# Two layers of a hybrid decoder on one core: parameter loads, a gate, a value half, the turnings and the warm-up put at other places

## The chip, the core and the metric

The kernel runs on one core of one Trainium2 chip. The time is that of the device in microseconds (us); runs of the same kernel are compared by their median. Five engines work beside each other, each through its own instructions in order: TensorE (PE: matmuls; PEld: the loading of their stationary operand), VectorE (DVE), ScalarE (ACT), GpSimd (POOL) and SyncE (SP), which here issues every DMA.

## What is computed

The input is 512 positions of width 1024 in float32. Two layers follow each other, each with `x <- LayerNorm(alpha * x + sublayer(x))`.

The first, even layer projects x to six parts (q, k, v, a gate g_ret, and xb, g_lru) and has two branches:

```
q, k = rope(q), rope(k) * dk**-0.5                # 8 heads of 128
ret  = (q k^T * decay) v                          # per head, causal
ret  = groupnorm(ret) * gn_g + gn_b;  ret *= silu(g_ret)
xc   = causal_conv4(xb)
r, i = sigmoid(xc Wa + ba), sigmoid(xc Wx + bx)   # 8 diagonal blocks
a    = exp(-8 r softplus(-lam));  u = xc i sqrt(1 - a^2)
lru  = scan(h = a h + u) * silu(g_lru)
y    = concat(ret, lru) W_out
```

The second, odd layer is differential attention with 8 heads, two softmax maps each:

```
w   = softmax(q1 k1^T) - lambda softmax(q2 k2^T)  # causal
out = rmsnorm(w v) * subln_g * (1 - lambda_init) * silu(g)
y   = out W_out
```

## The kernel before, in words

**Numbers.** Every matmul operand of weight is a pair: a rounded high part (`h`, cast by ScalarE) and the remainder (`l`, subtracted by VectorE). `split` (L140) makes such a pair, and `mm3` (L149) multiplies two pairs with three matmuls, high by high, high by low and low by high. So a product needs first the high parts and then the low ones.

**Weights.** They come in pieces of 128 x 1024 (512 KB), in the order of the list `order`, and are numbered w0, w1, ... in the profile. `fetch` (L164) loads the next piece into one of two raw buffers and splits it into one of five pairs; a raw buffer is free again when VectorE has made the low part. `take` (L179) hands out the next piece and fetches ahead. The arrays on the host are laid out in the same order (`layout`, L731).

**Units.** TensorE's main work is in units of 24 matmuls or 96: `t_unit` (a weight piece times all of x, result transposed: q, k, xb, and the gates gl and gr of the even layer), `s_unit` (four pieces, result by position: the values and the odd layer's gate og) and `out_unit` (the output projections: out, lo, ro, eo, oo). The even layer's order is the list `ev` (L249): for each pair of heads gl, xb, gr, q, k of the first head and then of the second, with the first half of the values (v 0, heads 0 to 3) ahead of all and the second half (v 1, heads 4 to 7) between xb 4 and gr 4. v 0 goes piece by piece; v 1 is "major": it takes its four pieces at once and goes position block by position block, and each block is evicted by `evac` (L415).

**Side work.** What a head does beside the projections is a generator: `retention` (L432), `lru` (L475), `attention` (L598), and the turning of the normalized rows (`fin`, L574). `Side` (L47) holds them as jobs. After each mm3 of a main unit one tick is counted (`side.tick`), and at each tick the first job that is due and within its group's limit runs one step, up to its next `yield n`, which makes it due n ticks later. TensorE's and SP's instructions stand in the program exactly in this order. Where a main unit needs a job's result, `side.need` puts the clock of ticks forward to the job's times and runs its steps at once, with no main matmuls in between. ScalarE's, VectorE's and GpSimd's instructions are ordered by a planner that goes by priorities.

Steps that the change and the prediction speak of:

- In `retention`: four scores `rs` (jb 0 to 3; 512, 384, 256, 128 columns) into two PSUM banks `ps_sc`, each multiplied by the decay into `rsd` and split; the product `ro` with the values; its square `rq`, split; after RET_NORM ticks the mean square `rv` through a matmul with `ones`; then the group norm and the gate. A head is in `seen` once its `ro` is in the program. Before v 1, the loop waits with `need` until heads 0 to 3 are in `seen` (L535), because v 1 is written over v 0's tiles.
- In `lru`: the convolution (xbp, xc); after LRU_GATES ticks the two gate products `pr` and `pi` at once, both into `ps_sc`; sigmoid of both (L492, L496), a tanh (L498), and so on to the scan.
- In `attention`, for one head and one block of 128 queries (qb): the scores `as` of the two maps, a masked maximum and exponentials; after ATT_SCORES ticks the turning `wt` of the weights; after ATT_TURN ticks the product `po` with the values, in the only bank of `ps_av`; a square sum (L638), its inverse root on GpSimd (L326, L327), the scaling to `o` on VectorE (L642); after ATT_NORM ticks two transposes (the turning of o, L646) into the free half of the same bank, split into `om`. ATT_FREE = 2 ticks later the next `po` may start. A head's blocks start at least ATT_GAP ticks apart (8; for the last head 7), three at a time.
- `ln_params` (L362) loads gain and offset of a normalization, broadcast over the partitions, in four halves of 256 KB. For the even layer that is at L568, behind `ident` and ahead of the last four weights of the layer (w60 is fetched already, w61 to w63 are not); the buffers are those of two decay tiles and of the gate weights.
- The start (L278 to L300): seven dummy matmuls on `ones`, then x and the first pieces, in turns.

Of the kernel before, what the change touches and what calls it, by code (L numbers as in the profile page):

```python
# [14 lines left out]
P = 128  # L15
D = 1024
S = 512
KT = D // P
SB = S // P
HALF = 512  # L20
# [12 lines left out]
ATT_START, ATT_GAP = (12,) * 7 + (7,), (8,) * 7 + (7,)  # L33
ATT_SCORES = (7, 7, 7, 9)
ATT_TURN = (4, 3, 4, 4)
ATT_NORM = 5
ATT_FREE = 2
ATT_VALUE = 2

P_ROPE, P_SCORES, P_SQUARE, P_GROUP, P_VALUE = 50, 13, 60, 5, 60  # L40
P_CONV, P_GATES = 9, 5
P_LN, P_LAST, P_WEIGHTS, P_ATT = 10, 10, 450, 337
WARM_UP = 7
EARLY = 2


# [50 lines left out]
def trunk(ctx: ExitStack, tc: tile.TileContext, a):  # L97
    nc = tc.nc
# [20 lines left out]
    side = Side()  # L119
# [17 lines left out]
    def cut(t, *ix):  # L137
        return t[0][ix], t[1][ix]
# [7 lines left out]
        nc.scalar.copy(out=dst[0], in_=src)  # L146
        nc.vector.tensor_tensor(out=dst[1], in0=src, in1=dst[0].bitcast(F32), op=ALU.subtract)

    def mm3(out, l, r, start, stop):  # L149
        nc.tensor.matmul(out=out, lhsT=l[0], rhs=r[0], start=start, stop=False)  # L150
        nc.tensor.matmul(out=out, lhsT=l[0], rhs=r[1], start=False, stop=False)  # L151
        nc.tensor.matmul(out=out, lhsT=l[1], rhs=r[0], start=False, stop=stop)  # L152

# [5 lines left out]

    ew, ow, eo, oo = a["ev_w"], a["od_w"], a["ev_wo"], a["od_wo"]  # L160
    order, ready = [], []
    extra, stats = {}, {}

    def fetch(parts=((0, D),)):  # L164
        if len(ready) < len(order):
            n = len(ready)
            src, scale = order[n]
            raw = wraw.tile([P, D], F32, tag="raw", name=f"w{n}_r")
            w = pair(extra.pop(n, wsp), [P, D], "w", f"w{n}")
            for lo, hi in parts:  # L170
                c = slice(lo, hi)
                nc.sync.dma_start(out=raw[:, c], in_=src[:, c])
                split(raw[:, c], cut(w, ALL, c), scale=scale)
                yield
            ready.append(w)

    taken = [0]
# [15 lines left out]
    def s_unit(act, name, major, evac, before=None):  # L193
        def product(ps, w, sb, kt):
            j = kt % 2 * HALF
            mm3(ps, cut(act, ALL, kt, slice(sb * P, sb * P + P)), cut(w, ALL, slice(j, j + HALF)), kt == 0, kt == KT - 1)
            if kt == KT - 1:
                evac(sb, ps)
            side.tick()

        if major:
            with tc.high_priority(P_WEIGHTS):
                ws = [take(0) for _ in range(KT // 2)]
            for sb in range(SB):
                before(sb)
                ps = bank(ps_pj, "pj", f"{name}_ps{sb}")
                for kt in range(KT):
                    product(ps, ws[kt // 2], sb, kt)
        else:
            ps = [bank(ps_pj, "pj", f"{name}_ps{sb}") for sb in range(SB)]  # L210
            for i in range(KT // 2):
                w = take(2)
                steps = [(sb, j) for sb in range(SB) for j in range(2)]
                if taken[0] == 1:

                    steps.sort(key=lambda t: t[1])
                for sb, j in steps:
                    product(ps[sb], w, sb, 2 * i + j)
# [30 lines left out]
    ev = [("v", 0)]  # L249
    for p in range(3):  # L250
        one, two = (2 * p, 2 * p + 1)
        ev += [("gl", one), ("xb", one)] + [("v", 1)] * (p == 2) + [("gr", one), ("q", one), ("k", one)]
        ev += [("gl", two), ("xb", two)] + [("out", p - 1)] * (p > 0) + [(n, two) for n in ("gr", "q", "k")]
    ev += [("xb", 6), ("q", 6), ("k", 6), ("lo", 2), ("xb", 7), ("q", 7), ("k", 7)]
    ev += [("gr", 6), ("gl", 6), ("gr", 7), ("gl", 7), ("ro", 2)]
# [26 lines left out]
    ones = const.tile([P, P], F32R, tag="ones", name="ones")  # L282
    nc.vector.memset(ones.bitcast(F32), 1.0 / P)
    idle = bank(ps_tp, "tp", "idle")
    for _ in range(WARM_UP):
        nc.tensor.matmul(out=idle, lhsT=ones, rhs=ones.unsqueeze(1).to_broadcast([P, 4, P]), start=True, stop=True)

    x = pair(big, [P, KT, S], "x", "x")
    xr = big.tile([P, KT, S], F32, tag="y", name="xr")
# [69 lines left out]
            nc.vector.scalar_tensor_tensor(out=hv[hf], in0=hv[hf], scalar=rs, in1=gb[1][hf], op0=ALU.mult, op1=ALU.add)  # L359
            yield hf, hv[hf]  # L360

    def ln_params(src, name, *slots):  # L362
        slots = iter(slots)
        return [[load(f"{name}{r}{hf}", [P, HALF], src[r:r + 1, hf * HALF:hf * HALF + HALF].partition_broadcast(P), *next(slots))
                 for hf in range(2)] for r in range(2)]


    phase = ctx.enter_context(ExitStack())
# [43 lines left out]
    def v_even(i):  # L412
        out = []

        def evac(sb, ps):  # L415
            with tc.high_priority(P_VALUE):
                p3 = ps.rearrange("p (h e) -> p h e", e=P)
                m = small.tile([P, 4], F32, tag="vm", name="vm")
                nc.vector.tensor_reduce(out=m, in_=p3, axis=AX.X, op=ALU.add)
                nc.vector.tensor_scalar(out=m, in0=m, scalar1=1.0 / P, scalar2=None, op0=ALU.mult)  # L420
                c = work("vc")
                nc.vector.tensor_tensor(out=c.rearrange("p (h e) -> p h e", e=P), in0=p3, in1=m.unsqueeze(2).broadcast_to([P, 4, P]), op=ALU.subtract)
                t = pair(vp, [P, S], "v", f"ev{i}{sb}")
                split(c, t)
            out.append(t)

        s_unit(x, f"ev{i}", i == 1, evac, lambda sb: None)
        return out
# [46 lines left out]
    def lru(c, ps, m):  # L475
        with tc.high_priority(P_CONV):
            xb = temp(f"xbp{c}")
            nc.scalar.copy(out=xb, in_=ps)
            xc = temp(f"xc{c}")
            nc.scalar.activation(out=xc, in_=ps, func=AF.Identity, scale=conv_w(3, c), bias=conv_b(c))  # L480
            for w in range(3):
                sh = 3 - w
                nc.vector.scalar_tensor_tensor(out=xc[:, sh:], in0=xb[:, :S - sh], scalar=conv_w(w, c), in1=xc[:, sh:], op0=ALU.mult, op1=ALU.add)  # L483
        with tc.high_priority(P_GATES):
            t2 = part(S, f"xc{c}")
            split(xc, t2)
        yield LRU_GATES[c]
        pr = bank(ps_sc, "sc", f"pr{c}")
        o = c % 2 * 2 * P
        mm3(pr, cut(gw[0], ALL, slice(o, o + P)), t2, True, True)  # L490
        t = temp(f"t{c}")
        nc.scalar.activation(out=t, in_=pr, func=AF.Sigmoid, bias=gba(c))  # L492
        pi = bank(ps_sc, "sc", f"pi{c}")
        mm3(pi, cut(gw[0], ALL, slice(o + P, o + 2 * P)), t2, True, True)
        i = xb
        nc.scalar.activation(out=i, in_=pi, func=AF.Sigmoid, bias=gbx(c))  # L496

        nc.scalar.activation(out=t, in_=t, func=AF.Tanh, scale=sp4[:, c:c + 1])  # L498
        nc.vector.tensor_tensor(out=i, in0=i, in1=xc, op=ALU.mult)  # L499
        d = xc  # L500
        r = temp(f"r{c}")

        nc.scalar.activation(out=r, in_=t, func=AF.Ln, bias=1.0)
        nc.scalar.activation(out=r, in_=r, func=AF.Exp, scale=-1.0)  # L504
        nc.vector.scalar_tensor_tensor(out=d, in0=t, scalar=1.0, in1=r, op0=ALU.add, op1=ALU.mult)  # L505
        nc.vector.scalar_tensor_tensor(out=d, in0=d, scalar=2.0, in1=r, op0=ALU.subtract, op1=ALU.mult)
        nc.scalar.activation(out=r, in_=t, func=AF.Sqrt)
        nc.vector.scalar_tensor_tensor(out=t, in0=t, scalar=1.0, in1=d, op0=ALU.subtract, op1=ALU.mult)
        nc.vector.scalar_tensor_tensor(out=r, in0=r, scalar=-2.0, in1=d, op0=ALU.mult, op1=ALU.mult)
        nc.vector.tensor_tensor(out=r, in0=r, in1=i, op=ALU.mult)  # L510
        nc.vector.tensor_tensor_scan(out=d, data0=t, data1=r, initial=0.0, op0=ALU.mult, op1=ALU.add)
        if ("gl", c) not in gates:
            yield lambda: 0 if ("gl", c) in gates else math.inf
        nc.vector.tensor_tensor(out=d, in0=d, in1=gates.pop(("gl", c)), op=ALU.mult)
        split(d, cut(m, ALL, c % 2))
# [17 lines left out]

    for kind, i in ev:
        if kind == "v":  # L535
            if i:
                for j in range(4):
                    side.need(job["ret", j], lambda: j in seen)
            v = v_even(i)
        elif kind == "xb":  # L540
            if i % 2 == 0:
# [23 lines left out]
    for i in (6, 7):  # L565
        side.need(job["lru", i])
    ident = load("ident", [P, P], a["ident"])
    gb0 = ln_params(a["ev_ln"], "ln0", (two, "dec"), (two, "dec"), (two, "gwh", 1), (two, "gwl", 1))  # L568
    h = pair(big, [P, KT, S], "x", "h")

    def even_end(sb):
# [26 lines left out]
    def attention(hd, qb, q, k, m):  # L598
# [37 lines left out]
        with tc.high_priority(P_ATT):  # L636
# [3 lines left out]
            rsqrt(ss, rs, 1.0 / (2 * P), zr[:, 1:2])  # L640
            o = es.tile([P, 2 * P], F32, tag="o", name=f"o{hd}{qb}")
            nc.vector.scalar_tensor_tensor(out=o, in0=po[:, :2 * P], scalar=rs, in1=gates[qb, hd // 2][:, hc:hc + 2 * P], op0=ALU.mult, op1=ALU.mult)  # L642
        yield ATT_NORM
        pm = po[:, 2 * P:]
        for i in range(2):
            nc.tensor.transpose(out=pm[:, i * P:i * P + P], in_=o[:, i * P:i * P + P], identity=ident)  # L646
# [27 lines left out]
    for kind, i in od:  # L674
# [31 lines left out]
                oj[i, qb] = side.add(attention(i, qb, *qk, om[i]), "att", 3, ATT_START[i], ATT_GAP[i])  # L706
        else:
            odd_out(i, f"oo{i[0]}")
    gb1 = ln_params(a["od_ln"], "ln1", *((qkp, n) for n in ("qh", "ql", "kh", "kl")))
    odd_out((6, 7), "oo6", after=odd_end, late=P_LAST)  # L710


# [18 lines left out]
def layout(i):  # L731
# [13 lines left out]
    for p in range(4):  # L745
        for h in (2 * p, 2 * p + 1):
            names = (wl, wx, wg, wq, wk) if p < 3 else (wx, wq, wk)
            part = [t_pieces(m[:, h * P:h * P + P]) for m in names]
            if h == 0:
                part.insert(0, s_pieces(wv[:, :HALF]))  # L750
            if h == 4:
                part.insert(2, s_pieces(wv[:, HALF:]))
            ev += part
    ev += [t_pieces(m[:, h * P:h * P + P]) for h in (6, 7) for m in (wg, wl)]
    w = i["od_w_in"][0]
# [38 lines left out]
```

## Time and profile before

| | |
|---|---|
| median of 3 runs | 938.7 us (938.13 to 939.02) |
| the profiled execution | 939.08 us, span 937.3 us |
| PE busy | 922.1 us, 4327 matmuls |
| DVE, ACT, POOL busy | 703.2, 450.6, 60.5 us |
| granted TensorE clock, mean | 0.997 |
| HBM read, written | 86.09 MB, 2.10 MB |

The span goes from the first to the last instruction of the profiled execution. In a timeline's row stand the start, the time taken, the engine, the line, the operation, and the tile written with the tiles read; "x2" means that two such instructions are merged. In brackets stands how long the engine was idle before, and the instruction that ended it. In a row of the waits stand the waiting engine and line, what it waited for, and the total, the number of times and the longest. `SPq` is SP issuing a DMA.

### The profile page before, as it was taken

What the parts mean: (1) busy time and instruction counts of PE and PEld (TensorE: products, weight loads), DVE (VectorE), ACT (ScalarE), POOL (GpSimd) and SP (SyncE); (2) the same over time, 40 slices, a digit from 0 to 9 for tenths busy, and PEclk for the clock granted to TensorE, in tenths of its full rate; (3) what the DMA queues carried; (4) which work ended last, traced back from release to release, by engine and by line L of the source; (5) the groups of instructions that cost most, each with busy time, mean ns of one, the idle gap of its engine ahead of it and who ended that gap; (6) DMA issues with size and microseconds to landing.
All of it is one profiled execution on the core that took longest, in us unless ns stands there. A gap on an engine that the chain in (4) does not pass through costs nothing.

```text
span 937.3 us, 11561 instructions
## 1 busy us (share of the span) xinstructions
PE 922.1 (98%) x4327; PEld 765.1 (82%) x4327; DVE 703.2 (75%) x1187; ACT 450.6 (48%) x740; POOL 60.5 (6%) x118
## 2 busy tenths in 40 slices
PE   9999999999999999999999999999999999999996
PEld 7888888878888887788888888888888888888885
DVE  6877997868769987994589864578764488647677
ACT  5567786566484776423334443233443234434240
POOL 0000000000000000000001210100110101101023
PEclk9999999999999999999999999999999999999998
DMA  6562221512314123405222122142222142223102
GB/s 226 179 215 68 88 75 53 168 57 90 124 41 161 57 90 115 124 3 188 90 91 68 68 88 73 43 133 92 69 68 90 45 135 68 69 90 112 67 23 91
DMA packets 27416, 88.94 MB, mean 95 GB/s; under 512 B 3424, under 2 KB 3552, under 8 KB 27360
## 3 DMA queue, kind: packets, MB, share of 16 engines
q1 hardware_dynamic: 27360, 88.20, 28.4%
q8 instruction: 34, 0.56, 0.2%
q14 instruction: 22, 0.18, 0.1%
HBM read 86.09 MB, written 2.10 MB: 94 GB/s over the span
## 4 chain that ended last, share of the span: by engine, by line
PE 74%; DVE 14%; ACT 6%; issue 3%; POOL 1%; DMA 1%; SPq 0%; DVEq 0%; ACTq 0%; POOLq 0%
PE ov_ps L152 3%; PE ov_ps L151 3%; PE ov_ps L150 3%; PE og_ps L150 3%; PE og_ps L152 3%; PE og_ps L151 3%; PE oo_ps L150 3%; PE oo_ps L151 2%; PE oo_ps L152 2%; PE ev_ps L150 2%; PE ev_ps L151 2%; PE ev_ps L152 2%; PE xb_ps L150 1%; PE xb_ps L151 1%; PE xb_ps L152 1%
## 5 line engine op out<-in xcount | busy, mean ns | idle before, releaser
L611 ACT ACTIVATE e<-as,nm 128x128 f32<-128x128 f32 (+3 forms) x64 | 33.1, 523 | 25.3 <-DVE nm L608 25.2
L642 DVE SCALAR_TENSOR_TENSOR o<-po,ars,og 128x256 f32<-128x256 f32 x32 | 15.5, 484 | 36.1 <-POOL ars L327 35.1
L618 POOL TENSOR_SCALAR zr<-z 128x1 f32<-128x1 f32 x32 | 13.4, 419 | 311.3 <-ACT e L611 311.3
L608 DVE CUSTOM_DVE_ANT_0 as<-as,mask 128x128 f32<-128x128 f32 (+3 forms) x64 | 30.2, 510 | 1.5 <-PE as L152 1.5
L326 POOL TENSOR_SCALAR rs_t<-bmv 128x1 f32<-128x1 f32 x6 | 2.2, 374 | 420.5 <-DVE bmv L337 420.5
L638 ACT ACTIVATE po<-po 128x256 f32<-128x256 f32 x32 | 11.9, 372 | 25.8 <-PE po L152 25.4
L326 POOL TENSOR_SCALAR rs_t<-ss,zr 128x1 f32<-128x1 f32 x32 | 14.9, 467 | 131.1 <-ACT po L638 126.0
L327 POOL TENSOR_TENSOR ars<-rs_t,nhalf 128x1 f32<-128x1 f32 x32 | 20.6, 644 | 2.7
L240 DVE TENSOR_TENSOR y<-oo_ps,y 128x512 f32<-128x512 f32 x24 | 16.4, 685 | 4.2 <-PE oo_ps L152 4.2
L483 DVE SCALAR_TENSOR_TENSOR xc<-xbp,vecs,xc 128x509 f32<-128x509 f32 (+2 forms) x24 | 17.9, 746 | 1.8 <-ACT xc L480 1.6
L619 DVE SCALAR_TENSOR_TENSOR e<-e,zr,e 128x128 f32<-128x128 f32 (+3 forms) x32 | 17.6, 551 | 0.9
L440 DVE TENSOR_TENSOR rsd<-rs,dec 128x512 f32<-128x512 f32 (+3 forms) x32 | 15.5, 486 | 1.0 <-PE rs L152 0.8
L646 PEld LDWEIGHTS po<-ident,o 128*128 128x128 f32 x64 | 8.3, 140 | 7.4 <-DVE o L642 4.5
L697 DVE SCALAR_TENSOR_TENSOR og<-og,og_ps 128x512 f32<-128x512 f32 x16 | 10.9, 686 | 4.3 <-ACT og L696 4.3
L623 PE MATMUL wt<-ident,e 128*128 128x128 f32 x80 | 13.9, 272 | 0.0
L646 PE MATMUL po<-ident,o 128*128 128x128 f32 x64 | 12.6, 278 | 1.1 <-DVE o L642 0.8
L696 ACT ACTIVATE og<-og_ps 128x512 f32<-128x512 f32 x16 | 9.6, 598 | 8.0 <-PE og_ps L152 7.7
L623 PEld LDWEIGHTS wt<-ident,e 128*128 128x128 f32 x80 | 10.5, 140 | 3.5
L146 ACT CAST hh<-ht 128x512 fp32r<-128x512 f32 x8 | 4.7, 588 | 17.5 <-PE ht L578 17.5
L499 DVE TENSOR_TENSOR xbp<-xbp,xc 128x512 f32<-128x512 f32 x8 | 5.5, 690 | 9.7 <-ACT xbp L496 9.7
L611 ACT ACTIVATION_READ_ACCUMULATOR e<-as,nm 128x1 f32 x64 | 12.6, 196 | 0.0
L505 DVE SCALAR_TENSOR_TENSOR xc<-t,r 128x512 f32<-128x512 f32 x8 | 5.5, 690 | 9.0 <-ACT r L504 9.0
(2672 smaller groups left out, 3409.3 us busy)
## 6 DMA issues: line engine op xcount, KB each, us to landing
w_r<-in_od_w SPq DMA_DIRECT2D x64, 512.0 KB, 3.3
w_r<-in_ev_w SPq DMA_DIRECT2D x47, 512.0 KB, 3.3
w_r<-in_ev_wo SPq DMA_DIRECT2D x16, 512.0 KB, 3.3
w_r<-in_od_wo SPq DMA_DIRECT2D x16, 512.0 KB, 3.3
dec<-in_dec SPq DMA_DIRECT2D x8, 256.0 KB, 3.8
y<-in_x SPq DMA_DIRECT2D x4, 512.0 KB, 6.7
out_h<-y SPq DMA_DIRECT2D x8, 256.0 KB, 2.1
xr<-in_xt SPq DMA_DIRECT2D x3, 512.0 KB, 6.9
```

The lines of the kernel that those rows point to most:

```text
L150: nc.tensor.matmul(out=out, lhsT=l[0], rhs=r[0], start=start, stop=False)
L151: nc.tensor.matmul(out=out, lhsT=l[0], rhs=r[1], start=False, stop=False)
L152: nc.tensor.matmul(out=out, lhsT=l[1], rhs=r[0], start=False, stop=stop)
L240: nc.vector.tensor_tensor(out=yy, in0=ps, in1=yy, op=ALU.add)
L326: nc.gpsimd.tensor_scalar(out=t, in0=var, scalar1=scale, scalar2=eps, op0=ALU.mult, op1=ALU.add)
L327: nc.gpsimd.tensor_tensor(out=out, in0=t, in1=nhalf[:, :1], op=ALU.pow)
L483: nc.vector.scalar_tensor_tensor(out=xc[:, sh:], in0=xb[:, :S - sh], scalar=conv_w(w, c), in1=xc[:, sh:], op0=ALU.mult, op1=ALU.add)
L608: nc.vector.tensor_tensor_reduce(out=ps[:, :n], in0=ps[:, :n], in1=mask[:, S - n:], scale=-QK_SCALE, scalar=3.0e38, op0=ALU.add, op1=ALU.m ...
L611: nc.scalar.activation(out=e, in_=ps[:, :n], func=AF.Exp, scale=-1.0, bias=nm, accum_out=z[:, mp:mp + 1])
L619: nc.vector.scalar_tensor_tensor(out=ee[0], in0=ee[1], scalar=zr[:, 0:1], in1=ee[0], op0=ALU.mult, op1=ALU.add)
L623: nc.tensor.transpose(out=pt[:, kb * P:kb * P + P], in_=ee[0][:, kb * P:kb * P + P], identity=ident)
L646: nc.tensor.transpose(out=pm[:, i * P:i * P + P], in_=o[:, i * P:i * P + P], identity=ident)
```

## The change

- The even layer's four parameter halves are no longer loaded together. `fetch` has a list `behind`: after a piece is fetched, what is listed for its number is run. The first half is listed behind the next piece, the second behind the one after it, the third and fourth behind the third.
- In `lru` a `yield 1` stands between `pr` and `pi`.
- In `ev`, for the pair p = 2, gr 4 comes ahead of v 1 (and so in `layout`). The `need` for heads 0 to 3 moves from before the value unit into its first eviction, which comes after eight of its mm3.
- ATT_NORM is 5, 6, 6, 6 for the query blocks 0 to 3 instead of 5 for all.
- WARM_UP is 8 instead of 7, and in the first mm3 of the kernel one more dummy matmul, of 256 columns, stands between the first and the second matmul (`between`).
- The odd layer's parameters are loaded as before, by another expression.

```diff
-ATT_NORM = 5
+ATT_NORM = (5, 6, 6, 6)
...
-WARM_UP = 7
+WARM_UP = 8
...
-    def mm3(out, l, r, start, stop):
+    def mm3(out, l, r, start, stop, between=lambda: None):
         nc.tensor.matmul(out=out, lhsT=l[0], rhs=r[0], start=start, stop=False)
+        between()
         nc.tensor.matmul(out=out, lhsT=l[0], rhs=r[1], start=False, stop=False)
...
-    extra, stats = {}, {}
+    extra, behind, stats = {}, {}, {}
...
                 split(raw[:, c], cut(w, ALL, c), scale=scale)
                 yield
+            for then in behind.pop(n, ()):
+                then()
             ready.append(w)
...
             j = kt % 2 * HALF
-            mm3(ps, cut(act, ALL, kt, slice(sb * P, sb * P + P)), cut(w, ALL, slice(j, j + HALF)), kt == 0, kt == KT - 1)
+            between = {"between": lambda: busy_pe(2)} if (taken[0], sb, kt) == (1, 0, 0) else {}
+            mm3(ps, cut(act, ALL, kt, slice(sb * P, sb * P + P)), cut(w, ALL, slice(j, j + HALF)), kt == 0, kt == KT - 1, **between)
...
-        ev += [("gl", one), ("xb", one)] + [("v", 1)] * (p == 2) + [("gr", one), ("q", one), ("k", one)]
+        ev += [("gl", one), ("xb", one), ("gr", one)] + [("v", 1)] * (p == 2) + [("q", one), ("k", one)]
...
+    def busy_pe(n):
+        nc.tensor.matmul(out=idle[:, :n * P], lhsT=ones, rhs=ones.unsqueeze(1).to_broadcast([P, n, P]), start=True, stop=True)
+
     for _ in range(WARM_UP):
-        nc.tensor.matmul(out=idle, lhsT=ones, rhs=ones.unsqueeze(1).to_broadcast([P, 4, P]), start=True, stop=True)
+        busy_pe(4)
...
-    def ln_params(src, name, *slots):
-        slots = iter(slots)
-        return [[load(f"{name}{r}{hf}", [P, HALF], src[r:r + 1, hf * HALF:hf * HALF + HALF].partition_broadcast(P), *next(slots))
-                 for hf in range(2)] for r in range(2)]
+    def ln_param(src, name, r, hf, slot):
+        return load(f"{name}{r}{hf}", [P, HALF], src[r:r + 1, hf * HALF:hf * HALF + HALF].partition_broadcast(P), *slot)
...
         def evac(sb, ps):
+            if i and sb == 0:
+                for j in range(4):
+                    side.need(job["ret", j], lambda: j in seen)
...
         nc.scalar.activation(out=t, in_=pr, func=AF.Sigmoid, bias=gba(c))
+        yield 1
         pi = bank(ps_sc, "sc", f"pi{c}")
...
         if kind == "v":
-            if i:
-                for j in range(4):
-                    side.need(job["ret", j], lambda: j in seen)
             v = v_even(i)
...
-    gb0 = ln_params(a["ev_ln"], "ln0", (two, "dec"), (two, "dec"), (two, "gwh", 1), (two, "gwl", 1))
+
+    gb0 = [[None] * 2, [None] * 2]
+    for n, slot in enumerate(((two, "dec"), (two, "dec"), (two, "gwh", 1), (two, "gwl", 1))):
+        def param(r=n // 2, hf=n % 2, slot=slot):
+            gb0[r][hf] = ln_param(a["ev_ln"], "ln0", r, hf, slot)
+
+        behind.setdefault(len(ready) + min(n, 2), []).append(param)
...
-        yield ATT_NORM
+        yield ATT_NORM[qb]
...
-    gb1 = ln_params(a["od_ln"], "ln1", *((qkp, n) for n in ("qh", "ql", "kh", "kl")))
+    gb1 = [[ln_param(a["od_ln"], "ln1", r, hf, (qkp, n)) for hf, n in enumerate(ns)] for r, ns in enumerate((("qh", "ql"), ("kh", "kl")))]
...
             if h == 4:
-                part.insert(2, s_pieces(wv[:, HALF:]))
+                part.insert(3, s_pieces(wv[:, HALF:]))
```

## The prediction

> **What bounds the kernel now.** I read the page's first two parts first, for the engine that is full, then what this engine waited for, and then the timeline around each of its waits.
>
> ```profile
> span 937.3 us, 11561 instructions
> ...
> PE 922.1 (98%) x4327; PEld 765.1 (82%) x4327; DVE 703.2 (75%) x1187; ACT 450.6 (48%) x740; POOL 60.5 (6%) x118
> ```
>
> TensorE is busy for 98% of the span, so nothing but its gaps can be won: 937.3 - 922.1 = 15.2 us, of which the normalization after the last matmul takes most. What the gaps wait for:
>
> ```profile
> PE rv L457 <- ACT rq7h L146: 1.4, 1, 1.4
> ...
> PE po L646 <- DVE o L642: 0.8, 2, 0.4
> PE pi L150 <- DVE rsd L440: 0.7, 1, 0.7
> ```
>
> A busy time here includes the drain of the pipeline, which is longer than the distance between two matmuls, so a gap shows up too small. I therefore measure from start to start: two 512-column matmuls at full clock start 0.23 us apart, a 384-column one takes 0.17 and a 256-column one 0.12 by the same proportion. All that is above this is lost time. A "tick" below is what one call of side.tick stands beside: three such matmuls, 0.68 us.
>
> **Part 1, the start (two more dummy matmuls).**
>
> ```profile
> 1.07 3.36 PE L286 MATMUL idle<-ones 128*128 128x512 f32 x7 [1.07 <-DVE ones L283]
> 4.92 0.80 PE L150 MATMUL ev_ps<-w0h,xh 128*128 128x512 f32 x1 [0.50 <-ACT w0h L146]
> 5.65 0.80 PE L151 MATMUL ev_ps<-w0l,xh 128*128 128x512 f32 x1
> 9.22 0.63 PE L150 MATMUL ev_ps<-w0h,xh 128*128 128x512 f32 x1
> 9.65 0.45 PE L151 MATMUL ev_ps<-w0l,xh 128*128 128x512 f32 x1
> 11.43 1.23 DVE L147 TENSOR_TENSOR w1l<-w_r,w1h 128x1024 fp32r<-128x1024 f32 x1 [0.41 <-ACT w1h L146]
> 12.90 0.39 PE L150 MATMUL ev_ps<-w1h,xh 128*128 128x512 f32 x1
> 13.13 0.39 PE L151 MATMUL ev_ps<-w1l,xh 128*128 128x512 f32 x1
> ```
>
> Up to 9.65 us matmuls start 0.43 us apart (9.22 to 9.65), after it 0.23: TensorE runs at half speed until it has worked without a break from 5.65 on, 4.0 us. Seven dummies at 0.43 are issued by 1.07 + 3.0 = 4.1; an eighth ends at 4.5 and so lies in the idle time before 4.92. The dummy between the first two real matmuls has 256 columns, 0.21 us at the slow rate, and stands in the 0.73 - 0.43 = 0.30 us that the second one waits for w0l. Both cost nothing while these waits are there; without them 0.43 and 0.21. What they may bring is that the busy stretch counts from 1.07 instead of from 5.65, so that full speed comes some 4.6 us earlier. But the data don't come earlier: the second matmul on w1 needs w1l, done at 11.43 + 1.23 = 12.66. It started at 13.13, so at most 0.47 us is won, and a loss is excluded as long as the waits stay. Ends 0 and 0.47; I take **0.4**, since the idle time left in the stretch (4.5 to 4.92, and 0.1) is short against what there was. By the Trainium skill (TensorE: Matmul & The Clock Gate, section "What's actually happening") the gate opens after one busy window of about 3.4 us, and the window is free-running. The trace's 4.0 us agrees. By that rule other runs of the kernel before turn fast up to 12.5 us (estimate: 5.65 and two windows), 1.4 us worse than this one, and the sum below would be up to 1.4 us better.
>
> **Part 2, value half 1 after gr4, and its need inside the first eviction.** The stretch in which the loop forced head 3's steps, each without cover, and the nearest like pattern (head 1):
>
> ```profile
> 191.63 0.29 PE L152 MATMUL rs<-q3h,k3l 128*128 128x256 f32 x1
> 192.20 0.33 PE L150 MATMUL rs<-q3h,k3h 128*128 128x128 f32 x1 [0.28 <-DVE rsd L440]
> 193.34 0.33 PE L150 MATMUL ro<-r31h,ev01h 128*128 128x384 f32 x1
> 194.13 0.44 PE L151 MATMUL ro<-r31l,ev01h 128*128 128x384 f32 x1 [0.46 <-DVE r31l L147]
> ...
> 122.14 0.50 PE L457 MATMUL rv<-rq1h,ones 128*128 128x512 f32 x1
> 122.87 0.50 PE L458 MATMUL rv<-rq1l,ones 128*128 128x512 f32 x1 [0.23 <-DVE rq1l L147]
> ```
>
> Lost: 0.57 - 0.12 = 0.45 and 0.79 - 0.17 = 0.62, together 1.07. After the change head 3's scores come by their own times (yields of 4, 4, 4, 7): one in xb4, two in gr4, the last at tick 1 of the value unit, and the product ro would be due at tick 8, which is where the need now stands. So it forces at most that one step, after seven ticks of cover, and the 1.07 go. Nothing is moved in the sum of work; the four weights of this unit and gr4's change places, equal in size, and q4 takes gr4's place as the unit whose next weight comes late. What comes in: lru 4's gates, due 12 ticks after their convolution, fall on ticks 6 and 7 with ro at 8 and rv six ticks later. That is head 1's pattern, where the second rv came 0.73 - 0.23 = 0.50 late. Bounds of this cost: 0, and 1.0 (twice that row, as the value evictions also want ScalarE there). I take 0.5: net **0.6** won.
>
> **Part 3, pi a tick behind pr.** Eight moves; one of them stands at a wait:
>
> ```profile
> 304.23 0.40 PE L152 MATMUL pr<-xc6h,gw6l 128*128 128x512 f32 x1
> 304.72 0.56 DVE L440 TENSOR_TENSOR rsd<-rs,dec 128x384 f32<-128x384 f32 x1
> 305.33 0.50 PE L150 MATMUL pi<-xc6h,gw6h 128*128 128x512 f32 x1 [0.71 <-DVE rsd L440]
> ```
>
> pi waits for its bank, which the multiply at 304.72 frees at 305.28. Lost: 1.10 - 0.23 = 0.87. With a tick of main matmuls (0.68) in front, 0.2 is left: **0.67** won. The other seven cost TensorE nothing, they only change places with three matmuls. ScalarE does the tanh of pr's gate before pi's sigmoid in most of them (L498 ahead of L496), and that covers the tick; uncovered, each gate would come up to 0.68 later on ScalarE.
>
> **Part 4, the norm parameters one by one behind w61, w62, w63.**
>
> ```profile
> 356.47 10.46 SPq L156 DMA_DIRECT2D ln<-in_ev_ln  x4
> 367.04 8.72 SPq L172 DMA_DIRECT2D w_r<-in_ev_wo  x3
> ...
> 365.54 1.22 DVE L147 TENSOR_TENSOR w59l<-w_r,w59h 128x1024 fp32r<-128x1024 f32 x1
> ...
> 373.10 1.05 ACT L146 CAST w61h<-w_r 128x1024 fp32r<-128x1024 f32 x1 [6.64 <-DMA w_r<-in_ev_wo]
> ...
> 373.54 0.39 PE L152 MATMUL ro_ps<-w59h,retm2l 128*128 128x512 f32 x1
> 375.35 0.50 PE L457 MATMUL rv<-rq7h,ones 128*128 128x512 f32 x1 [1.42 <-ACT rq7h L146]
> 376.08 0.50 PE L458 MATMUL rv<-rq7l,ones 128*128 128x512 f32 x1 [0.22 <-DVE rq7l L147]
> ...
> w_r<-in_ev_wo SPq DMA_DIRECT2D x16, 512.0 KB, 3.3
> ```
>
> Four broadcasts of 256 KB stand in SP's queue before w61; the last are issued just ahead of it. w61 needs 6.06 us to 373.10, against a median of 3.3. ScalarE works in order, so the cast of w61 holds up head 7's square and cast, and with them rv: 1.81 - 0.23 = 1.58 and 0.73 - 0.23 = 0.50, together 2.08 lost. Moving the loads doesn't issue w61 much earlier, because its raw buffer is w59's, free at 365.54 + 1.22 = 366.76. What goes is the competition: landed after 3.3 us, w61 is there at 370.2, and cast, square and cast (some 2.4 us in all) end at 372.6, ahead of the 373.77 at which TensorE wants rv. The first parameter now follows w61 at once. If the two share the engines, w61 lands 0.7 us later (the excess of 6.06 - 3.3 = 2.8 spread over four loads) to 1.4 (over two); with 0.7 its low half and then rq7l still come in time, with 1.4 rq7l is 0.6 late. I take 0.2: **1.9** won, bounds 0.5 (the cast only half as much earlier) and 2.08. By the Trainium skill (DMA: Bandwidth & Descriptors, "Queues, rings and completion order") descriptors of one queue are consumed in ring order, which would make the later load harmless and the sum 0.2 better. Of what is queued behind the parameters on SP: w62, w63, lq and w64. The second parameter's slot is head 7's decay, whose last multiply is done before w59l, and the last two take lru 7's gate weights, long used; so none of them waits in the queue by then. The normalization that reads them comes after the whole first row of eo; if they were late there, up to their 3.9 us each could be lost.
>
> **Part 5, one tick more before the turning (query blocks 1 to 3).**
>
> ```profile
> 504.76 0.39 PE L152 MATMUL q20o_ps<-hh,w80l 128*128 128x512 f32 x1
> 505.23 0.44 PE L646 MATMUL po<-ident,o 128*128 128x128 f32 x2
> ...
> 675.56 0.39 PE L152 MATMUL og_ps<-w105h,hl 128*128 128x512 f32 x1
> 676.38 0.44 PE L646 MATMUL po<-ident,o 128*128 128x128 f32 x2 [0.42 <-DVE o L642]
> ...
> 866.83 0.19 PEld L150 LDWEIGHTS po<-ov30h,w63h 128*128 128x128 f32 x1 [0.47 <-DVE om6l L147]
> ```
>
> The turning waits for VectorE's o, which waits for GpSimd. Lost at 505: 0.47 - 0.23 = 0.24; at 676: 0.82 - 0.23 = 0.59. I find seven such places, two like the second (676, 806) and five of 0.21 to 0.25 (505, 515, 558, 666, 795), none of them in query block 0: 1.17 + 1.14 = 2.3. One tick, 0.68, is more than the longest. What it costs: the single bank of po is free one tick later. So the distance between two po of a head is 6 + 2 = 8 ticks, which is ATT_GAP; before it was 7. Counted through by hand, most heads keep their starts (a collision at tick 24 even lets the next head start a tick earlier), and head 1's four po come to stand right at the end of the bank's two free ticks, where the row at 866 shows a wait of about 0.2 us. Two of these four I count: 0.4. Bounds 0 and 0.8. Net **1.9** won.
>
> **Part 6, the end.** Head 7's turnings come 0, 1, 2 and 3 ticks later. Its last one stands at tick 43 of the drain and the last row of oo6 begins behind tick 49; 46 is in time.
>
> ```profile
> 917.00:929.00 12.00, 11.69 (x53) 9.32 (x51) 11.73 (x22) 1.14 (x2) 3.02 (x5) 1.00 0.13 48
> 917.10 0.48 DVE L642 SCALAR_TENSOR_TENSOR o<-po,ars,og 128x256 f32<-128x256 f32 x1 [1.60 <-POOL ars L327]
> ```
>
> The columns of the first row are stretch, length, then PE, PEld, DVE, ACT and POOL busy. VectorE is busy 11.73 of the last 12 us, and the o of head 7 still lies in an idle time ahead of that. Two ticks later it lies in it: 0.48 more on an engine without slack, at the end of which the kernel ends. Bounds 0 and 0.9 (with the split behind it); I take **0.4 lost**.
>
> **Sum.** 0.4 + 0.6 + 0.67 + 1.9 + 1.9 - 0.4 = 5.1 us. The profiled execution took 939.08 for its span of 937.3, the median of the runs is 938.7, so it stands 0.4 above. I take the sum off the median: **933.6 us**.
>
> **Rivals.** (a) The gains are partly handed on: clock no earlier, rv3 and the banks of po at their upper ends, w61 only halfway. 0 + 0.1 + 0.67 + 0.5 + 1.5 - 0.4 = 2.4 won, 936.3; for it speaks how closely VectorE and ScalarE follow TensorE, against it that each of these ends needs its own bad luck. (b) Hidden anyway: ScalarE and VectorE are ordered by a planner, and a new order puts as many small waits elsewhere as go; 938.3 (only the 0.4 of the start). Against it: the long waits each have one named cause that is taken away. (c) Slower: the drain of head 7. With 8 ticks between its po against a gap of 7, the place where it decides is tick 49: if collisions push the last two turnings beyond it, the need of the last row runs them without cover, 5 ticks of 0.68 = 3.4 us each, and VectorE's full stretch takes 0.9 more: 7.7 - 5.5 = 2.2 lost, 940.9. Against it: three ticks of slack are left by my count.
>
> **How the numbers follow.** Forecast 0.64 (its own range 931.5 to 935.4), (a) 0.17, (b) 0.12, (c) 0.07. The bounds of the parts give 931 at best (2.08 + 2.3 + 1.07 + 0.87 + 0.47 + 1.4 = 8.2 less small costs), so the range goes from 930.9 to 937.4 and leaves out (b), (c) and little else. A difference within 0.2% (936.8 to 940.6) cannot be told from none. Faster: the forecast and most of (a), 0.78; same: (b) and the rest of (a), 0.15; slower 0.07.
>
> **What would show it.** In TensorE's waits rv from rq7h, pi from rsd and po from o are gone or under 0.2; w61's cast starts before 371.5 less what was won before; matmuls are 0.23 apart before 8 us and the second one on w1 starts at about 12.7; no gap between the last score of head 3 and its ro; a new wait at rv for rq3l. Wrong would make it: a new wait of po for om, a last turning right before the last row, or matmuls at half speed up to 9.65 as before.

## The result and the profile after

| | before | after |
|---|---|---|
| median of 5 runs each | 938.73 us (938.13 to 939.44) | 944.59 us (944.04 to 946.01) |
| ratio | | 1.0065 (95% interval 1.0051 to 1.008) |
| span of the profiled execution | 937.3 us | 942.5 us |

The changed kernel is 5.9 us slower; 933.6 was predicted, and the range ended at 937.4. In the changed kernel some lines have moved: `rv` is L466 and L467, the decay's multiply L449, the scaling to o L655, the turning of o L659, the second and third matmul of an mm3 L152 and L153. One run of the kernel before, taken beside e1 to e4, lasted 1019.45 us at a granted clock of 0.851 and is left out of every comparison.

The page of the changed kernel, span and busy times:

```profile
span 942.5 us, 11557 instructions
...
PE 922.2 (98%) x4329; PEld 764.9 (81%) x4329; DVE 702.6 (75%) x1187; ACT 450.2 (48%) x739; POOL 57.6 (6%) x118
```

No engine is busy for more than 0.1 us longer than before. So the 5.2 us of span are time in which TensorE stands still, or runs slowly. What TensorE waits for in the changed kernel (total, times, longest, in us):

```profile
PE po L150 <- DVE om1l L147: 3.0, 3, 1.8
PE po L150 <- DVE om0l L147: 1.5, 1, 1.5
...
PE po L153 <- DVE w03l L147: 0.9, 1, 0.9
...
PE rv L467 <- DVE rq3l L147: 0.6, 1, 0.6
...
PE po L150 <- DVE om6l L147: 0.4, 1, 0.4
```

The waits of before that the prediction named are gone: `rv` for rq7h (1.4), `pi` for rsd (0.7), the turning for o (0.8 in two). In their place `po` waits for `om`, the split of the turned rows, four times in head 1, and the last product of head 0 waits for its own weights w03 (0.9 here, and 0.3 for their high part). To see where the time goes I compared the starts of the same matmuls in the two timelines (after less before, us):

| up to | after - before |
|---|---|
| gl 3 (w19) | -0.51 |
| gr 3 (w25) | +0.47 |
| behind the second half of the values (w35) | +0.23 |
| behind lru 6's gates (w49) | -0.49 |
| behind head 7's rv (w60) | -2.50 |
| the gates and first keys of the attention (w80) | -2.39 |
| behind head 1 (w90) | +5.85 |
| behind the second group of heads (w116) | +4.94 |
| behind the third (w132) | +4.02 |
| last matmul | +3.99 |
| end of the span | +5.2 |

Up to the attention the change had won 2.4 us. Between 505 and 565 us it lost 8.2, the second and third group won 0.9 each, and the end lost 1.2. The stretch with the loss by windows (stretch, length, busy time of PE, PEld, DVE, ACT, POOL, granted TensorE clock, DMA share, GB/s), first of the kernel before:

```profile
520.00:560.00 40.00, 40.00 (x216) 33.94 (x215) 29.57 (x65) 18.18 (x46) 8.78 (x14) 1.00 0.20 67
```

and of the changed kernel, the same stretch and pieces of it:

```profile
520.00:560.00 40.00, 35.03 (x177) 28.52 (x178) 27.44 (x59) 14.55 (x40) 5.35 (x12) 0.96 0.19 61
...
535.00:540.00 5.00, 3.23 (x18) 2.48 (x17) 4.57 (x9) 2.65 (x8) 0.27 (x1) 1.00 0.00 0
540.00:542.00 2.00, 2.00 (x7) 1.46 (x6) 1.20 (x3) 0.33 (x2) 1.27 (x2) 0.54 0.19 51
542.00:544.00 2.00, 2.00 (x8) 1.65 (x7) 0.87 (x2) 0.48 (x1) 0.00 (x0) 0.60 0.53 211
```

TensorE was busy throughout before; now it stands still for 5.0 of 40 us, and after the stalls it runs at about half clock from 540.3 to 543.5.

How this comes about is seen in the order of four kinds of steps: `as` (scores of head 1), `po<-ident,o` (the turning), `po<-ov..` (the next product in the same bank), and the split `om`. The timeline before, at the seam from head 0 to head 1:

```profile
515.34 0.44 PE L646 MATMUL po<-ident,o 128*128 128x128 f32 x2
...
517.45 0.22 PE L150 MATMUL as<-k10oh,q10oh 128*128 128x128 f32 x1
...
525.16 0.38 PE L646 MATMUL po<-ident,o 128*128 128x128 f32 x2
...
526.08 0.28 PE L150 MATMUL as<-k10oh,q10oh 128*128 128x256 f32 x1
...
528.18 0.28 PE L150 MATMUL po<-ov00h,w10h 128*128 128x256 f32 x1
```

and in the changed kernel:

```profile
513.13 0.22 PE L150 MATMUL as<-k10oh,q10oh 128*128 128x128 f32 x1
...
514.49 0.38 PE L659 MATMUL po<-ident,o 128*128 128x128 f32 x2
...
523.30 0.27 PE L150 MATMUL as<-k10oh,q10oh 128*128 128x256 f32 x1
...
526.50 1.04 ACT L146 CAST w87h<-w_r 128x1024 fp32r<-128x1024 f32 x1
...
526.76 0.38 PE L659 MATMUL po<-ident,o 128*128 128x128 f32 x2
...
527.44 0.38 ACT L146 CAST om0h<-po 128x256 fp32r<-128x256 f32 x1
...
528.81 0.68 DVE L320 TENSOR_TENSOR k20o_s<-k20o_ps,sin 64x512 f32<-64x512 f32 x1
...
529.53 0.42 DVE L147 TENSOR_TENSOR om0l<-po,om0h 128x256 fp32r<-128x256 f32 x1
...
530.01 0.39 PE L150 MATMUL po<-ov00h,w10h 128*128 128x256 f32 x1 [1.48 <-DVE om0l L147]
...
538.75 0.39 PE L150 MATMUL po<-ov00h,w11h 128*128 128x256 f32 x1 [1.77 <-DVE om1l L147]
```

Before, head 0's turnings stood ahead of head 1's scores at both places, since a tick runs one step, and pushed them back: counted in ticks, head 1's blocks followed each other at 9, not at the 8 of ATT_GAP. Now the turnings come one and two ticks later and the scores run first; head 1 starts two ticks earlier against head 0 and runs at 8. Its first `po` stood 3 ticks behind the last turning of head 0 before and the next ones 4 and 5 behind their own; now all four stand 2 behind, the least that ATT_FREE allows. Two ticks are 1.4 us, and the split takes longer than that here: the cast stands on ScalarE behind a weight's cast (1.04 us), the subtraction on VectorE behind the rotation of the next keys. In the row at 529.53 the subtraction starts 1.7 us after the cast is done; three operations of VectorE (two of the rotation, one on e) run in between. Two ticks are enough at most other places: in the kernel before, 13 `po` stand two ticks behind a turning, and only the one at 866 us waits.

### The profile page after: what moved, and what is told of

It is laid out like the page before. It is cut to its first block, busy times and chain, and to the rows that moved or that the text cites. A ratio compares the mean times of both kernels' runs of the same rounds, so it can differ in the third digit from the quotient of the medians.

```text
span 942.5 us, 11557 instructions
## 1 busy us (share of the span) xinstructions
PE 922.2 (98%) x4329; PEld 764.9 (81%) x4329; DVE 702.6 (75%) x1187; ACT 450.2 (48%) x739; POOL 57.6 (6%) x118
## 4 chain that ended last, share of the span: by engine, by line
PE 81%; DVE 9%; ACT 4%; issue 2%; DMA 2%; POOL 1%; SPq 0%; POOLq 0%; DVEq 0%; ACTq 0%
PE ov_ps L153 3%; PE ov_ps L152 3%; PE ov_ps L150 3%; PE og_ps L150 3%; PE og_ps L152 3%; PE og_ps L153 3%; PE oo_ps L150 3%; PE oo_ps L152 3%; PE oo_ps L153 3%; DMA w_r<-in_ev_w 2%; PE gr_ps L150 1%; PE gr_ps L152 1%; PE gr_ps L153 1%; PE q_ps L150 1%; PE q_ps L153 1%
## 5 line engine op out<-in xcount | busy, mean ns | idle before, releaser
L655 DVE SCALAR_TENSOR_TENSOR o<-po,ars,og 128x256 f32<-128x256 f32 x32 | 15.5, 484 | 42.6 <-POOL ars L335 41.7
L631 POOL TENSOR_SCALAR zr<-z 128x1 f32<-128x1 f32 x32 | 9.9, 308 | 283.4 <-ACT e L624 283.4
L629 DVE RECIPROCAL zr<-z 128x1 f32<-128x1 f32 x32 | 5.2, 163 | 14.9 <-ACT e L624 14.8
L449 DVE TENSOR_TENSOR rsd<-rs,dec 128x512 f32<-128x512 f32 (+3 forms) x32 | 15.5, 485 | 0.9 <-PE rs L153 0.9
L636 PEld LDWEIGHTS wt<-ident,e 128*128 128x128 f32 x80 | 10.7, 143 | 3.7 <-issue 0.2
L659 PEld LDWEIGHTS po<-ident,o 128*128 128x128 f32 x64 | 9.0, 140 | 4.2
L659 PE MATMUL po<-ident,o 128*128 128x128 f32 x64 | 12.2, 271 | 0.0
```

What stands on the lines that cost most here:

```text
L636: nc.tensor.transpose(out=pt[:, kb * P:kb * P + P], in_=ee[0][:, kb * P:kb * P + P], identity=ident)
```

## The experiments

Times are medians; runs of the kernel before on the same chip and beside them gave 938.71 us (e1 to e4), 938.48 (e5 to e8) and 938.64 (e9 to e12).

**The turnings or the rest (e1, e2, e3).** e1 is the changed kernel with the old turnings, e2 the kernel before with the new turnings, e3 the changed kernel with the new turnings in heads 3 to 6 only.

```diff
e1:  -ATT_NORM = (5, 6, 6, 6)
     +ATT_NORM = (5, 5, 5, 5)
e2:  kernel before;  -ATT_NORM = 5
     +ATT_NORM = (5, 6, 6, 6)
e3:  -        yield ATT_NORM[qb]
     +        yield ATT_NORM[hd][qb]      # (5, 6, 6, 6) for hd 3 to 6, else (5, 5, 5, 5)
```

> Theory 1 (the later turnings hold the only bank of po, so that head 1's products each stand right behind the two free ticks and wait for om's split): with 5 ticks for all blocks the waits of po for om between 518 and 558 us go (6.7 us from start to start) and so does the half clock at 540 to 543 (1.6 us); the waits of po for o come back (2.3 us). What was won up to the first attention step (2.4 us) stays: 936.3 us. Theory 2 (one of the other edits, the value half or the parameter loads, disturbs the order of VectorE and ScalarE later on): still about 944 us.

> Theory 1: the kernel before with nothing but the turnings changed loses what the changed kernel lost behind its first attention step, 6.4 us up to the last matmul and 1.2 behind it: 946.3 us. Theory 2: the turnings alone win the 1.9 us of the prediction, 936.8 us.

> Heads 0 to 2 and 7 turn after 5 ticks, heads 3 to 6 after 5, 6, 6, 6. Theory 1: no bank waits in the first three heads, the two pairs of later heads keep the waits of po for o away (0.9 each), the end is that of the kernel before: 934.5 us. If instead the later heads only won because the first ones had lost before them, it comes out with 5 ticks for all, 936.3.

Measured: e1 936.91 us (936.50 to 937.79), ratio 0.9982 (0.9972 to 0.9991); e2 944.79 (944.47 to 946.17), ratio 1.0066 (1.005 to 1.0082); e3 934.95 (934.59 to 935.23), ratio 0.9959 (0.9944 to 0.9974). The waits of e2 are those of the changed kernel:

```profile
PE po L150 <- DVE om1l L147: 3.0, 3, 1.7
PE po L150 <- DVE om0l L147: 1.5, 1, 1.5
```

So the loss is the turnings' alone: they cost 944.59 - 936.91 = 7.7 us on top of the rest and 944.79 - 938.71 = 6.1 on their own. In the groups of heads 3 to 6 the same edit wins 936.91 - 934.95 = 2.0. In head 3 the next head's scores move ahead of the turning just as in head 0, but there nothing follows: head 4's values come later, and its first `po` starts 29 us behind head 3's last turning (685.46 and 714.61 us in e3). Head 1 is the only head whose values are there when its predecessor still turns.

**One more free tick (e4).** The changed kernel with the bank held a tick longer, so that the main matmuls cover the split.

```diff
-ATT_FREE = 2
+ATT_FREE = 3
```

> The changed kernel with three free ticks between a turning and the next po. Theory 1: each wait of po for om shrinks by one tick, 0.68 us (1.64 to 0.96, 1.94 to 1.26, 0.96 to 0.28, 0.58 to 0), the half clock at 540 goes; head 1's last turning is then forced by the og unit at 2.7 ticks and costs 1.5 again: 941 us. Rival (VectorE is full there and TensorE would wait for it in any order): the waits keep their sum, about 944 us.

Measured once: 939.32 us. Its waits:

```profile
PE po L659 <- DVE o L655: 1.5, 3, 0.6
...
PE po L150 <- DVE om1l L147: 0.5, 1, 0.5
...
PE po L150 <- DVE om0l L147: 0.4, 1, 0.4
```

The four waits (1.64, 1.94, 0.96 and 0.58 us from start to start) shrink to 0.51, 0.61, 0 and 0, the first two by more than the tick of 0.68 that I had expected, and TensorE keeps its full clock in this stretch. The forced last turning that I had expected at 1.5 us didn't come. 944.59 - 939.32 = 5.3 us come back, though nothing was changed but the time for which the bank is held, and the order that follows from it: the split's time against the ticks that cover it is the cause, and a longer turning chain as such is not. It is no remedy, since the order shifts again: three waits of the turning for o come back (in heads 0, 3 and 5), and it stays above e1.

**The other parts alone (e5, e6, e7).** Each is the kernel before with one part of the change.

```diff
e5:  parameter halves behind w61, w62 and w63, as in the change
e6:  v 1 behind gr 4, its need in the first eviction, as in the change
e7:  +        yield 1                     # between pr and pi
```

> The kernel before with nothing but the parameter loads moved. Theory (they compete with w61): w61's cast starts at 370.2 instead of 373.1 and both waits of rv for head 7 go, 1.2 to 2.1 us by the waits seen so far: 936.6 to 937.5 us. Rival (w61 is late because of its raw buffer alone): the cast stays at 373 and the time at 938.7.

> The kernel before with nothing but the value half moved. Theory of the prediction: the gaps at 191 to 195 us go (1.1 shown, 1.4 with the small ones) and rv of head 3 costs 0.5: 938.1. Second theory, after the changed kernel's trace: rv of head 3 costs 1.3 in this place, so nothing is left: 938.7.

> The kernel before with nothing but the tick between pr and pi. Theory: only the gap at 305 us shrinks, by 0.5 to 0.7, and no other gap comes: 938.1. Rival (the tick delays the gates and then the products that wait for ScalarE, at 122, 147 and 318 us): those gaps grow and the time is 938.7 or more.

Measured once each: e5 936.69 us, e6 938.53, e7 938.10, against 938.48 (937.86 to 939.16 in seven runs). The runs of one kernel lie up to 0.7 from their median here, so only e5's gain stands out in the time; the rest is read from the timelines, which show the same in these kernels as in the changed one. The parameters, in the changed kernel:

```profile
366.60 0.33 SPq L173 DMA_DIRECT2D w_r<-in_ev_wo  x1
366.98 0.43 SPq L157 DMA_DIRECT2D ln<-in_ev_ln  x1
...
369.90 1.05 ACT L146 CAST w61h<-w_r 128x1024 fp32r<-128x1024 f32 x1 [3.67 <-DMA w_r<-in_ev_wo]
...
373.50 0.39 PE L466 MATMUL rv<-rq7h,ones 128*128 128x512 f32 x1
373.50 0.19 PEld L467 LDWEIGHTS rv<-rq7l,ones 128*128 128x128 f32 x1
373.73 0.39 PE L467 MATMUL rv<-rq7l,ones 128*128 128x512 f32 x1
```

w61 lands 3.30 us after its issue, the two `rv` follow at 0.23, and the 2.1 us of before are gone. The parameter issued 0.38 us behind w61 doesn't slow it: the ring order that the prediction cited from the Trainium skill (DMA: Bandwidth & Descriptors, "Queues, rings and completion order") fits this. The value half, in the changed kernel:

```profile
210.53 0.49 PE L466 MATMUL rv<-rq3h,ones 128*128 128x512 f32 x1 [0.18 <-ACT rq3h L146]
...
211.67 0.50 PE L467 MATMUL rv<-rq3l,ones 128*128 128x512 f32 x1 [0.65 <-DVE rq3l L147]
```

From start to start 0.34 + 0.91 + 0.11 = 1.36 us are lost at head 3's `rv`; the gaps at 191 to 195 that went were 1.07 in the two waits named and 1.4 with the small ones beside them. VectorE makes the low half of a value block (ev10l) first, then rq3l. Little is left of this part: by the table of starts 0.47 - 0.23 = 0.24 us, too little for e6's one run to show. And `pi`:

```profile
304.46 0.40 PE L153 MATMUL pr<-xc6h,gw6l 128*128 128x512 f32 x1
...
305.50 0.50 PE L150 MATMUL pi<-xc6h,gw6h 128*128 128x512 f32 x1
```

The two are 1.04 us apart: 0.23, a tick of 0.68, and 0.13 left of the 0.87. Later the product ro of head 5 waits some 0.2 longer than before, in e7 too.

**Which head (e9, e10, e11).** The changed kernel with the new turnings in one head alone; the yardstick is e1's 936.91.

```diff
-        yield ATT_NORM[qb]
+        yield ATT_NORM[hd][qb]            # (5, 6, 6, 6) for hd 0 (e9), 1 (e10), 7 (e11), else (5, 5, 5, 5)
```

> The changed kernel with the six-tick turnings in head 0 alone (all other heads 5). Measured against the changed kernel with 5 in every head, 936.9 us. Theory (head 0's third turning, a tick later for each query block, puts head 1's first po right behind the turnings of head 0's last block in the same bank): the waits at 518 us (0.46 + 1.08) and some of head 1's four (1.64 + 1.94 + 0.96 + 0.58) stay, with the half clock of about 1.6, so 940 to 943. Rival (head 1's own later turnings hold the bank, and head 0 only gains its waits for the attention operands): 936.9 or a little less.

> The changed kernel with the six-tick turnings in head 1 alone. Theory (the loss lies at the seam from head 0 to head 1): no waits of po for the eviction of the turnings in head 1, 936.5 to 937. Rival (head 1's own later turnings hold the bank): the four waits stay, 940 to 943.

> The changed kernel with the six-tick turnings in head 7 alone. Theory (what head 7's two more pushed ticks cost is all at the end: 1.2 us more behind the last matmul): 938.1. Rival (the longer tail of the changed kernel comes from the whole shift of VectorE's work before): 936.9.

Measured: e9 944.56 us (943.61 and 945.51), ratio 1.0063 (1.0043 to 1.0083); e10 937.78 (937.12 to 938.49), ratio 0.9992 (0.9982 to 1.0002); e11 938.33 (937.68 to 938.75), ratio 0.9996 (0.9986 to 1.0006). The waits of e9:

```profile
PE po L150 <- DVE om1l L147: 3.2, 2, 1.8
PE po L150 <- DVE om0l L147: 1.5, 1, 1.5
```

Head 0 alone costs 7.7 us by the median of two runs 1.9 apart, as much as the whole loss and above what I had expected: three `po` of head 1 stand two ticks behind a turning though head 1's own turnings are the old ones. Head 1 at 5 ticks needs its bank for 7 of 8, so it catches up, after the third; with 6 it needs 8 of 8, and in the changed kernel the fourth waits too. Head 1 alone has no such wait. It costs 0.9, by two waits that I had not foreseen, the turning of the weights for e:

```profile
PE wt L636 <- DVE e L632: 0.6, 2, 0.3
```

Head 7 alone costs 1.4 by the medians; by the traces 1.16 of it come behind the last matmul. The last steps in e1, with the old turnings:

```profile
926.01 0.39 PE L153 MATMUL oo_ps<-w143h,om7l 128*128 128x512 f32 x1
926.44 0.69 DVE L244 TENSOR_TENSOR y<-oo_ps,y 128x512 f32<-128x512 f32 x1
...
928.18 1.26 POOL L359 TENSOR_TENSOR y<-y,ln 128x512 f32<-128x512 f32 x1
...
929.40 0.99 POOL L350 TENSOR_TENSOR lrs<-lve,nhalf 128x1 f32<-128x1 f32 x1
```

and in e11:

```profile
926.26 0.39 PE L153 MATMUL oo_ps<-w143h,om7l 128*128 128x512 f32 x1
...
927.36 0.68 DVE L244 TENSOR_TENSOR y<-oo_ps,y 128x512 f32<-128x512 f32 x1
...
929.15 1.81 POOL L359 TENSOR_TENSOR y<-y,ln 128x512 f32<-128x512 f32 x1
...
930.93 0.99 POOL L350 TENSOR_TENSOR lrs<-lve,nhalf 128x1 f32<-128x1 f32 x1
```

VectorE's last addition starts 1.10 instead of 0.43 us behind the last matmul, and GpSimd's addition of the offset takes 1.81 instead of 1.26 (in e11 VectorE's next instruction, L365, starts 0.04 us ahead of it, in e1 0.03 behind it). All 14 traces show this pair: where VectorE starts first (the changed kernel, e2, e4, e11), GpSimd's addition takes 1.80 to 1.81 us; where GpSimd starts first (the other ten), it takes 1.26, and VectorE's instruction takes 1.77 to 1.79 instead of 0.74. So each slows the other, by the order in which they start; no run changed that order alone. The addition stands ahead of the last inverse root, which comes 1.28 later against the last matmul.

**A better version (e8, e12).** The new turnings in heads 3 to 5 only, and the mean square of head 3 (e8), in e12 of head 1 too, two ticks later.

```diff
e8:  -RET_NORM = (8, 6, 8, 6, 8, 6, 5, 5)
     +RET_NORM = (8, 6, 8, 8, 8, 6, 5, 5)
e12: +RET_NORM = (8, 8, 8, 8, 8, 6, 5, 5)
```

> The changed kernel with the later turnings for heads 3 to 5 alone and with rv of head 3 two ticks later (8 instead of 6). Theory: against the kernel with heads 3 to 6 (934.95) the wait of po for om at 856 shrinks by 0.4 and the wait of rv at 211 goes, 1.36: 933.2 us. Rival (rv two ticks later holds its bank longer and the wait comes out elsewhere): 934.6.

> The six-tick turnings in heads 3 to 5 alone, rv of units 0 to 3 issued at its latest place (8). Theory (rv1's two waits at 122 us, 0.50 + 0.11, go as rv3's did): 934.0 - 0.6 = 933.4. Rival (a later rv holds its bank longer, or the wait comes back in the next unit): 934.0 or more.

Measured: e8 933.97 us (933.41 to 934.22), ratio 0.9949 (0.9932 to 0.9965), faster than both kernels and the best of all, though 0.8 above the 933.2 expected (head 3's waits of rv went; a wait of 0.50 for k71ol at 875 us, which e3 didn't have, came back); e12 935.86 (934.78 to 936.77), ratio 0.9969 (0.9956 to 0.9981). In e12 the two waits of rv1 are gone, as theory had it, but head 1's normalized rows come later too, and the output projection `out` waits for them, e12's timeline:

```profile
141.07 0.50 PE L150 MATMUL out_ps<-w24h,retm0h 128*128 128x512 f32 x1 [0.91 <-ACT retm0h L146]
...
142.81 0.50 PE L153 MATMUL out_ps<-w24h,retm0l 128*128 128x512 f32 x1 [1.01 <-DVE retm0l L147]
...
144.09 0.63 PE L150 MATMUL out_ps<-w24h,retm0h 128*128 128x512 f32 x1
144.51 0.63 PE L152 MATMUL out_ps<-w24l,retm0h 128*128 128x512 f32 x1
```

The rival held: the wait came back in the next unit, 1.08 + 1.17 from start to start, and with it matmuls 0.43 apart from 143.7 to 146.6.

## Why the prediction was wrong

**Part 5 failed, by its price.** Its gain is right: all waits of the turning for o are gone in the changed kernel. The step that failed is "Two of these four I count: 0.4. Bounds 0 and 0.8." The place was named and the ticks were right, all four `po` of head 1 stand two ticks behind a turning. But the price was taken from one row at 866 us, 0.2. There one VectorE operation of 0.68 us (the low half of q71o, from 865.75) stood ahead of the subtraction; at 527 to 529 us there were three, and the four waits came to 5.1 instead of 0.4. That these operations are the reason is read from the timelines; no run moved them. Two more terms had no place in the sum at all: the wait for w03 and the half clock. Against e1 the changed kernel loses:

| | us |
|---|---|
| four `po` of head 1 for om: 1.64 + 1.94 + 0.96 + 0.58 | 5.1 |
| `po` of head 0's last block for w03: 0.46 + 1.08 | 1.5 |
| half clock behind the stalls | 1.6 |
| a `po` of head 6 for om6l (865 us), 0.57 instead of 0.21 | 0.4 |
| the end | 1.2 |
| less the waits of the turning that went, as predicted | -2.3 |
| sum (difference of the spans, 942.5 - 935.0) | 7.5 |

The second row has the same origin: the turning of w03 comes a tick later behind head 0's turning, its cast then stands behind that of w86, and its low half behind the rotation.

The sentence "before it was 7" about the distance of two `po` hid the slack. 7 was what the bank needed; what the heads used was 9, because turnings and scores met in a tick. I noted the collision that "even lets the next head start a tick earlier" as a small gain, when it was what took the slack.

**Part 6** had the mechanism and the wrong size: 1.2 in the traces of the changed kernel and of e11 instead of 0.4, above its bound of 0.9. VectorE's last addition comes 0.67 later, within the bound; the 0.55 that GpSimd's addition takes longer was left out of the sum.

**Part 4** is right: 2.2 in this timeline, 1.8 in e5's one run, against 1.9. The wait that it removes varies by itself: 1.58 in the profile before, 0.68 to 0.88 in e2, e6 and e7, which keep the old loads, each with 0.50 behind it. So the gain lies anywhere between 1.2 and 2.1 in these four executions.

**Part 3** is right: 0.74 of the 0.87 went, and 0.22 came back at ro; 0.5 net against 0.67.

**Part 2** was mis-sized. The gaps went, but `rv` of head 3 costs 1.36 instead of 0.5, above the bound of 1.0; net 0.24, and e6 shows no gain.

**Part 1** is not to be seen in the time. In the nine profiles with the two dummies the granted clock is full from 4.1 to 7.2 us on; in the five without from 4.6 and 4.9 in two (e7, e5) and from 9.4 to 10.7 in three. So the reading that TensorE must first work 4.0 us without a break was made from one profile and doesn't hold: e7 got its full clock behind the seven old dummies, before the first weight. The second matmul on w1 starts at 13.26 us on average with the dummies (12.28 to 13.73) and at 13.31 without (12.90 to 13.61). With them it waits for w1l each time, as the lower bound of the step said; without them it does in three of five, and in the kernel before and e6 it starts 0.48 and 0.61 behind w1l's end. That much is won where the clock would have come late, but w1l itself is done anywhere between 12.23 and 13.68 us.

Parts 1 to 4 were to win 0.4 + 0.6 + 0.67 + 1.9 = 3.6; e1 won 1.8. A new wait of lru 3's `pr`, 0.80 in the changed kernel, was not foreseen; it is 0.3 to 0.5 in five of the other kernels with the same order, absent in e3, e9 and e12, and absent in all five kernels that have at most one part of the change. So the change seems to have a part in it; which one, no run shows.

**The rivals.** (a), gains partly handed on, fits parts 1 to 3, but not the sign. (c) had the right sign at the wrong place: no turning of head 7 ran uncovered, the bank decided in the first group. Nor was (b) true, a new order with as many small waits: the new waits are few, long and at one seam.

## What to carry over

Moving a step by one tick moves what it collides with: write down for each head the distance of its steps that the old order really used, not the least that it needs, and see whether the collision was what kept two users of one buffer apart. The price of a wait on an evicted buffer is to be read at the place where it will stand, with what lies ahead of the eviction on ScalarE and VectorE there, not from a row elsewhere. An edit that is right for some heads can be put in for these alone; in e8, with one more step moved, 4.5 us were won where the changed kernel lost 5.9.

## What was not expected of the hardware

TensorE fell to half clock behind stalls of which none was longer than 1.8 us: granted 0.54 and 0.60 after 3.23 of 5 us busy, and in e12 0.64 and 0.51 behind a stretch with 1.07 of 3 us busy, each time for 3.4 us. By the Trainium skill (TensorE: Matmul & The Clock Gate, section "What's actually happening") the slow state comes after an idle window of about 3.4 us; no stretch of that length was idle here.

The traces show what was enough. In each of them the changes of the granted clock lie whole multiples of 3.413 us apart (in the changed kernel at 4.28, 540.17, 543.58 and 936.12 us: 157, 1 and 115 of them), so each trace can be cut into windows of that length. The window ahead of the half clock, and the one with it, in the changed kernel (columns as above):

```profile
536.76:540.17 3.41, 1.64 (x10) 1.34 (x10) 3.35 (x6) 1.06 (x4) 0.00 (x0) 1.00 0.00 0
540.17:543.58 3.41, 3.41 (x12) 2.61 (x11) 1.90 (x4) 0.64 (x3) 1.27 (x2) 0.50 0.42 154
```

The 14 traces have 3772 such windows between the first full clock and the last matmul. In four of them TensorE is busy for less than half, 1.5 to 1.7 us (e12, the changed kernel, e9, e2), and just these four are followed by a window at half clock; the next emptiest, 1.93 in e9 and 2.01 in the changed kernel, are not. That answers why the stalls of 1.64 us at 530 us in the changed kernel and at 550 us in e9 had no such effect: their windows were busier. So it is not the length of a stall that decides here but the busy time of its window, and where the windows lie differs from run to run. The untraced runs fit this: e9 took 945.51 us at a mean granted clock of 0.996 and 943.61 at 0.998, e12 936.37 to 936.77 at 0.995 and 934.78 to 935.35 at 0.996 to 0.998; so part of the 1.6 us is chance. No run set out to test this, and the limit is only known to lie between 1.7 and 1.9 of 3.4 us.
